# A decoder layer on one core: the v branch turned by transposing DMAs instead of TensorE

## The chip, the cores and the metric

The kernel runs on one core of one Trainium2 chip. The core has a matrix engine (TensorE, in the profile PE, its weight loads PEld), VectorE (DVE), ScalarE (ACT), GpSimd (POOL), and SyncE (SP), which here only issues DMAs. Each engine takes its instructions strictly in the order in which they were written; semaphores hold one back until what it needs is there. Times are device microseconds of one execution.

## What is computed

One layer of a decoder trunk over 1024 prompt tokens and 8 sample tokens, 1024 channels, all float32. The part that matters here is branch A:

```
u, v, z_a, x_b, z_b, g_a, g_b = split(rmsnorm(h) @ w_in)      # 7 x 1024 columns
vn  = layernorm(gelu(v))                    # over the 1024 channels of a token
s   = tril(w_s[g]) @ vn + b_s               # per chunk of 128 tokens, group of 128 channels
y_a = gelu(u) * s * silu(z_a)
```

The rest (a pooling branch B, a gated merge, an output projection, a second gate with a per-layer embedding) follows behind it and is not touched. Two of the outputs are rows of `vn`.

## The kernel before

**Products.** Every projection has its channels on the partitions and the tokens along the free axis, which is how `x` is kept. A *pair* is 256 output channels, so each of the seven branches has four pairs. A pair is computed by one step of Strassen's scheme: seven products of 12 matrix blocks (names P1 to P7, and in the profile by their operand: B11, T2, B21, T3, T4, T1, B22). Each float32 operand is split into a high half (ScalarE, a rounding copy) and a low half (VectorE, a subtraction), and a product takes three of the four combinations. So for every product ScalarE makes a weight half (`vw` for v, `gaw` for the gate branch), VectorE the other, and the results, in PSUM regions `acc`, are evacuated by ScalarE (`u<-acc`, `v<-acc`) or added by VectorE. Three such regions rotate. The order of branches is V, GA (gate), then U and ZA by turns, then branch B.

**The v branch.** A pair of v is two tiles `v` of 128 channels x 1032 tokens. LayerNorm runs over channels and the chunk mixing multiplies over tokens, so v is turned to tokens on the partitions, in `big[:, t, :]`, one row of 1024 channels per token block t. `v_turn` does that: PE transposes 128x128 blocks into a PSUM bank `vt` (two blocks t by two tiles, four at a time), and ScalarE reads the bank, applies the GELU, writes `big` and sums along the way (`vsums`). The sample tokens are the ninth block, `[S]`, into the tile `sv`. `V.turns` lists the blocks that are turned after each of the following products: five groups for a pair. The LayerNorm (`ln_stats`, `ln_apply`), the split of its result (`v_split`) and the mixing on PE (`spatial`, tile `mix`; for the sample tokens `sample_spatial`, tile `smix`) follow in the gate branch, one token block every four products.

**What sets the order.** The kernel is not written to the engines directly. A `Planner` records every operation with an estimated duration and the product that it belongs to (`at(step, f)` hangs an operation behind a product). It then orders each engine's queue by due times, and writes the result out (the one line L293, which is why all rows of the profile have that line). Weights are prepared three products ahead (`AHEAD`). 46 buffers of equal size (`slot`) are handed round among all tiles. DMAs other than the adding ones on POOL are issued from SP's queue, in the planned order.

Of the kernel before, what the change touches and what calls it, by code (L numbers as in the profile page):

```python
# [8 lines left out]
F32 = mybir.dt.float32  # L9
F32R = mybir.dt.float32r  # L10
BF16 = mybir.dt.bfloat16
AF = mybir.ActivationFunctionType
ALU = mybir.AluOpType

P = 128
D = 1024
NB = D // P
SEQ = 1024
NS = 8
# [35 lines left out]
class Planner:  # L55
# [24 lines left out]

    def space(self, ap):

        dims, start = list(ap.ap), ap.offset
        if "DRAM" in str(ap.space):
            row = ap.tensor.shape[-1]
            first, start = divmod(start, row)
            rows = sum(s // row * (n - 1) for s, n in dims if s >= row)
            return (ap.tensor.name, first, first + rows + 1,
                    ((start, start + sum(s * (n - 1) for s, n in dims if s < row) + 1),))
        row, parts = dims[0]  # L90
        first, start = divmod(start, row)
        pieces = [(start, start + 1)]
# [35 lines left out]
    def duration(self, engine, method, out, reads, kwargs):  # L128
        n = out.free_size()
        if engine == "tensor":  # L130
            return 0.109 if method == "transpose" else max(0.06, 0.0062 + n / 2268)
        if engine == "vector":
            if method == "tensor_reduce":
                n = reads[0].free_size()
            quick = method in ("tensor_scalar", "tensor_scalar_mul", "tensor_copy")
            quick = quick and self.tags.get(reads[0].tensor.name) in (None, "slot")
            return 0.065 + n * (0.00059 if quick else 0.00105) + (0.06 if method[:8] == "scalar_t" else 0)
        if engine == "scalar":
            return max(0.09 + n * 0.00086, 0.26 if n > 1 else 0) + (0.2 if kwargs.get("accum_out") is not None else 0)
        return 0.1 + n * 0.0008 if method == "memset" else 1.0  # L140

    def take(self, engine, method, args, kwargs):
        given = [*(("out" if i == 0 else "", a) for i, a in enumerate(args)), *kwargs.items()]
        writes = [a for k, a in given if k in ("out", "accum_out") and a is not None]
        reads = [a for k, a in given if k not in ("out", "accum_out") and hasattr(a, "tensor")]
        if kwargs.get("accum_op") is not None:
            reads += writes
        name = writes[0].tensor.name
        if engine == "tensor" and self.open is not None and self.open[0] == name:
            op = self.open[1]  # L150
        else:
# [5 lines left out]
        if method == "dma_start":  # L157
            op.busy, op.moved = 1.0 if engine == "gpsimd" else 0.45, writes[0].size() * 4e-6
# [141 lines left out]
def hybrid_step(  # L300
# [7 lines left out]
    nc = tc.nc  # L308
# [53 lines left out]
    ident = cpool.tile([P, P], F32, tag="ident", name="ident")  # L362
# [6 lines left out]
    nc = plan  # L369
# [3 lines left out]
    big = cpool.tile([P, NB, T], F32, tag="big", name="big")  # L373
# [34 lines left out]
    class Operand:  # L408
# [37 lines left out]
        def at(self, what, k):  # L446
            return [part[:, k % 2, :] for part in self.parts[what, k // 2]]
# [237 lines left out]
    class User:  # L685

        func = AF.Copy

# [165 lines left out]
            mul(quarter(kp, 1)[:, :, HALF:], ps[:, 2 * kp : 2 * kp + 2, :NS], g.to_broadcast([P, 2, NS]))  # L854

    S = NB
    xop = Operand("x")
    inp = lambda c0, i: w_in[:, c0 + 2 * i * P : c0 + (2 * i + 2) * P]


    NPAIR = NB // 2
    vsums = cpool.tile([P, NB + 1, NPAIR], F32, tag="vsums", name="vsums")
    sv = slot("sv", (P, D))
    vtok = lambda t: sv if t == S else big[:, t, :D]

    def v_turn(out, pair, ts):

        if ts == [S]:
            ps = bank("vt")
            for m in range(2):  # L870
                nc.tensor.transpose(ps[:NS, m * P : (m + 1) * P], out[m][:, SEQ:T], ident)
            places = [(S, ps[:NS, : 2 * P], NS)]
        else:
            ps = bank("vt").rearrange("p (t c) -> p t c", t=2)
            for i, t in enumerate(ts):
                for m in range(2):
                    nc.tensor.transpose(ps[:, i, m * P : (m + 1) * P], out[m][:, t * P : (t + 1) * P], ident)
            places = [(t, ps[:, i], P) for i, t in enumerate(ts)]
        for t, src, n in places:
            nc.scalar.activation(out=vtok(t)[:n, 2 * pair * P : (2 * pair + 2) * P], in_=src,  # L880
                                 func=AF.Gelu_apprx_tanh, accum_out=vsums[:n, t, pair : pair + 1])

    class V(User):
        turns = [[0, 1], [2, 3], [4, 5], [6, 7], [S]]

    lnv = {}

# [373 lines left out]
    at(vsteps[1][2], spatial_weights)  # L1261
    for i, u in enumerate(vusers):

        nxt = vsteps[1][3:] if i == 0 else (vsteps[i + 1][1:] if i + 1 < NPAIR else gasteps[0][0:])
        if i == 0:
            nxt = vsteps[1][2:]
        for s, ts in zip(nxt, V.turns):
            at(s, lambda u=u, i=i, ts=ts: v_turn(u.out, i, ts))
    at(vsteps[3][0], ln_rows)
    flow = [s for p in gasteps for s in p] + [s for p in usteps[0] for s in p]  # L1270
    for n, t in enumerate([NB - 1, *range(NB - 1)]):
        s = 3 + 4 * n
# [46 lines left out]
    turn_over(ybop, l, [*l[1:], c[0]])  # L1319


    rows = lambda t: NS if t == S else P
# [390 lines left out]
```

## Time and profile before

| | |
|---|---|
| three runs | 1001.23, 1001.62, 1002.43 us; median 1001.62 |
| profiled execution, span | 1002.0 us |
| PE busy | 989.1 us, 99% |
| VectorE, ScalarE, GpSimd busy | 800.1, 490.0, 73.7 us |
| granted clock of TensorE, mean | 0.996 |
| DMA | 166.95 MB, mean 167 GB/s |

The profiled execution and the median of the runs lie 0.4 us apart. V's products of pairs 1 to 3 run from 65 to 136 us, the gate branch from 131 us on. A row of a timeline gives start, length, engine and operation, as `out<-in`; a row of the waits gives who waited for whom: total, times, longest; a row of the windows gives a stretch and the busy time of PE, PEld, DVE, ACT and POOL in it, the granted clock, the DMA share and GB/s.

### The profile page before, as it was taken

The page shows a single profiled execution, that of the slowest core. Times are in us where ns is not written, and L with a number is a line of the kernel's source. Part 1 is how long each engine was busy: PE and PEld are TensorE (multiplying, and loading weights), DVE is VectorE, ACT ScalarE, POOL GpSimd, SP SyncE. Part 2 cuts the span into 40 slices and gives each one's busy share as a digit, 9 for nine tenths or more (in the row PEclk, how much of TensorE's full clock was granted, in tenths as well). Part 3 has the DMA queues.
Part 4 walks back from the last instruction along what each step waited for, and adds up shares of the span by engine and source line. Part 5 has one row for each costly group of instructions (what it writes and reads, how often), then busy time and mean ns, then how long its engine had stood idle before and what let it go on. Part 6 is the DMA issues. An engine that isn't in the chain of part 4 may idle for free.

```text
span 1002.0 us, 16159 instructions
## 1 busy us (share of the span) xinstructions
PE 989.1 (99%) x6200; PEld 889.8 (89%) x6200; DVE 800.1 (80%) x1241; ACT 490.0 (49%) x891; POOL 73.7 (7%) x162
## 2 busy tenths in 40 slices
PE   8999999999999999999999999999999999999996
PEld 7889999999999999999999999999999988888885
DVE  5985448877788788788898887697799798779796
ACT  7664356556434343233433343552353365677653
POOL 2200001000000000000000100000000002312111
PEclk9999999999999999999999999999999999999998
DMA  9231214222364345637544166884573553389546
GB/s 353 117 121 43 84 43 129 85 85 86 101 235 169 127 167 183 210 127 252 200 158 143 61 222 244 266 305 148 199 268 107 177 201 71 80 275 364 160 109 188
DMA packets 87330, 166.95 MB, mean 167 GB/s; under 512 B 7614, under 2 KB 47598, under 8 KB 87245
## 3 DMA queue, kind: packets, MB, share of 16 engines
q1 hardware_dynamic: 84885, 158.01, 45.3%
q0 software_dynamic: 2048, 7.37, 4.3%
q8 instruction: 49, 0.80, 0.3%
q10 hardware_dynamic: 320, 0.54, 0.2%
q14 instruction: 28, 0.23, 0.1%
HBM read 114.59 MB, written 51.77 MB: 166 GB/s over the span
## 4 chain that ended last, share of the span: by engine, by line
PE 97%; DVE 1%; POOL 0%; issue 0%; ACT 0%; POOLq 0%; DVEq 0%
PE acc L293 71%; PE acct L293 15%; PE accm L293 2%; PE e L293 2%; PE sps L293 2%; PE mix L293 1%; PE vt L293 1%; PE pst L293 1%; PE pht L293 1%; PE warm L293 1%; DVE sv L293 0%; DVE ge L293 0%; PE smix L293 0%; PE state L293 0%; DVE welo L293 0%
## 5 line engine op out<-in xcount | busy, mean ns | idle before, releaser
L293 DVE TENSOR_TENSOR u<-acc,u 128x520 f32<-128x520 f32 (+1 forms) x90 | 62.5, 695 | 36.5 <-PE acc L293 35.0
L293 POOL TENSOR_TENSOR rstd<-ms,mhalf 128x1 f32<-128x1 f32 (+1 forms) x45 | 38.2, 851 | 204.8 <-DVE ms L293 182.5
L293 POOL MEMSET u<- 128x8 f32 x35 | 3.5, 105 | 556.1 <-PE acc L293 242.5
L293 ACT ACTIVATE u<-acc 128x512 f32<-128x512 f32 x39 | 23.2, 596 | 33.4 <-PE acc L293 33.1
L293 ACT ACTIVATE paw<-pas 128x512 fp32r<-128x512 f32 x16 | 10.0, 627 | 30.0 <-DVE pas L293 24.8
L293 ACT ACTIVATE pbw<-pbs 128x512 fp32r<-128x512 f32 x16 | 10.0, 629 | 29.1 <-DVE pbs L293 25.9
L293 DVE TENSOR_TENSOR big<-big 128x1024 f32<-128x1024 f32 (+4 forms) x20 | 23.6, 1215 | 0.0
L293 ACT ACTIVATE big<-vt 128x256 f32<-128x256 f32 x32 | 11.9, 380 | 21.4 <-PE vt L293 21.4
L293 ACT ACTIVATE big<-pht,gvec 128x128 f32<-128x128 f32 x64 | 18.0, 381 | 8.0 <-PE pht L293 8.0
L293 ACT ACTIVATE big<-mix 128x256 f32<-128x256 f32 x32 | 12.1, 383 | 19.0 <-PE mix L293 18.6
L293 PE MATMUL accm<-qh,wpoolw 128*128 128x260 f32 (+1 forms) x96 | 21.0, 320 | 0.0
L293 ACT ACT_TABLE_LOAD x13 | 16.7, 1283 | 4.6 <-PE acc L293 3.6
L293 DVE TENSOR_TENSOR v<-acc,u 128x520 f32<-128x520 f32 (+1 forms) x9 | 6.3, 697 | 14.9 <-PE acc L293 14.8
L293 DVE TENSOR_TENSOR acc<-acc,u 128x512 f32<-128x512 f32 (+1 forms) x16 | 11.1, 697 | 8.7 <-PE acc L293 8.7
L293 ACT ACTIVATE gbw<-gbs 128x512 fp32r<-128x512 f32 x16 | 10.0, 624 | 16.4 <-DVE gbs L293 13.8
L293 ACT ACTIVATE zaw<-zas 128x512 fp32r<-128x512 f32 x16 | 10.0, 628 | 14.9 <-DVE zas L293 10.6
L293 ACT ACTIVATE zbw<-zbs 128x512 fp32r<-128x512 f32 x16 | 10.1, 630 | 14.6 <-DVE zbs L293 7.3
L293 PEld LDWEIGHTS accm<-qh,wpoolw 128*128 128x128 f32 x96 | 15.5, 188 | 1.9
L293 DVE TENSOR_TENSOR big<-mix,big 128x256 f32<-128x256 f32 x32 | 13.2, 421 | 4.4 <-ACT big L293 3.5
L293 ACT ACTIVATE uw<-us 128x512 fp32r<-128x512 f32 x16 | 9.8, 627 | 13.7 <-DVE us L293 7.2
L293 ACT ACTIVATE zbw<-zbraw 128x512 fp32r<-128x512 f32 x12 | 7.5, 626 | 18.2 <-DMA zbraw<-in_w_in_dram 9.2
L293 ACT ACTIVATE gb<-gb 128x1032 f32<-128x1032 f32 (+1 forms) x8 | 6.8, 854 | 18.8 <-DVE gb L293 18.8
(687 smaller groups left out, 3629.8 us busy)
## 6 DMA issues: line engine op xcount, KB each, us to landing
ga<-ga SPq DMA_DIRECT2D x16, 516.0 KB
gb<-gb SPq DMA_DIRECT2D x16, 516.0 KB
ya<-za SPq DMA_DIRECT2D x8, 516.0 KB
yb<-zb SPq DMA_DIRECT2D x8, 516.0 KB
x<-in_x_prompt_dram SPq DMA_DIRECT2D x8, 512.0 KB
vraw<-in_w_in_dram SPq DMA_DIRECT2D x8, 512.0 KB
e<-e SPq DMA_DIRECT2D x8, 512.0 KB
garaw<-in_w_in_dram SPq DMA_DIRECT2D x8, 512.0 KB
```

What stands on the lines that cost most here:

```text
L293: getattr(getattr(self.nc, e), method)(*args, **kwargs)
```

## The change

PE no longer turns the prompt tokens of v. Instead, for each tile, ScalarE copies the 1024 f32 values of a partition, seen as pairs of two-byte words, into two planes `vw` (all low words, all high words: two operations, `v_planes`). One transposing DMA from SP turns the 16 blocks of 128x128 words of these planes and writes them over the tile's own bytes (`v`). ScalarE then joins the words into f32 values in `big`, four token blocks in each of two operations (`v_join`). The GELU now reads `big` and writes it in place. The sample tokens are still transposed by PE. The planes are made behind the first of the following products, the joins behind the third and fourth, the GELUs behind the fifth to seventh (`V.turns`); the sample's turn moves from the last of these places to the first. LayerNorm and mixing move back by two products. The planner counts space in bytes and has durations for the new operations.

```diff
+    def v_planes(out, pair):
+
+        for m in range(2):
+            words, v = slot("vw", (P, 2, SEQ), U16), out[m][:, :SEQ].bitcast(U16)
+            for w in range(2):
+                nc.scalar.activation(out=words[:, w], in_=v.rearrange("p (t w) -> p w t", w=2)[:, w], func=AF.Copy)
+            nc.sync.dma_start_transpose(out=v.rearrange("p (k c) -> p k c", c=P),
+                                        in_=words.rearrange("p w t -> p (w t)"))
+
+    def v_join(out, pair, m):
+
+        c = 2 * (2 * pair + m) * P
+        for j in range(2):
+            ts = slice(4 * j, 4 * j + 4)
+            nc.scalar.activation(out=big.bitcast(U16)[:, ts, c : c + 2 * P].rearrange("p t (c w) -> p t c w", w=2),
+                                 in_=out[m][:, :SEQ].bitcast(U16).rearrange("p (w t c) -> p t c w", w=2, c=P)[:, ts],
+                                 func=AF.Copy)
+
     def v_turn(out, pair, ts):
 
         if ts == [S]:
             ps = bank("vt")
             for m in range(2):
                 nc.tensor.transpose(ps[:NS, m * P : (m + 1) * P], out[m][:, SEQ:T], ident)
-            places = [(S, ps[:NS, : 2 * P], NS)]
-        else:
-            ps = bank("vt").rearrange("p (t c) -> p t c", t=2)
-            for i, t in enumerate(ts):
-                for m in range(2):
-                    nc.tensor.transpose(ps[:, i, m * P : (m + 1) * P], out[m][:, t * P : (t + 1) * P], ident)
-            places = [(t, ps[:, i], P) for i, t in enumerate(ts)]
-        for t, src, n in places:
-            nc.scalar.activation(out=vtok(t)[:n, 2 * pair * P : (2 * pair + 2) * P], in_=src,
-                                 func=AF.Gelu_apprx_tanh, accum_out=vsums[:n, t, pair : pair + 1])
+        for t in ts:
+            n, c = rows(t), slice(2 * pair * P, (2 * pair + 2) * P)
+            v = vtok(t)[:n, c]
+            nc.scalar.activation(out=v, in_=ps[:NS, : 2 * P] if t == S else v, func=AF.Gelu_apprx_tanh,
+                                 accum_out=vsums[:n, t, pair : pair + 1])
 
     class V(User):
-        turns = [[0, 1], [2, 3], [4, 5], [6, 7], [S]]
+        turns = [[7, 0, 1], [2, 3, 4], [5, 6]]
...
     for i, u in enumerate(vusers):
 
-        nxt = vsteps[1][3:] if i == 0 else (vsteps[i + 1][1:] if i + 1 < NPAIR else gasteps[0][0:])
-        if i == 0:
-            nxt = vsteps[1][2:]
-        for s, ts in zip(nxt, V.turns):
-            at(s, lambda u=u, i=i, ts=ts: v_turn(u.out, i, ts))
+        nxt = vsteps[1][1:] + vsteps[2] if i == 0 else (vsteps[i + 1] if i + 1 < NPAIR else gasteps[0])
+        at(nxt[0], lambda u=u, i=i: v_turn(u.out, i, [S]))
+        at(nxt[0], lambda u=u, i=i: v_planes(u.out, i))
+        for m in range(2):
+            at(nxt[2 + m], lambda u=u, i=i, m=m: v_join(u.out, i, m))
+        for s, ts in zip(nxt[4:], V.turns):
+            at(s, lambda i=i, ts=ts: v_turn(None, i, ts))
...
-        s = 3 + 4 * n
+        s = 5 + 4 * n
```

ScalarE's queue around the first tile of pair 0 (`vw_298`, `vw_303` and so on are weight halves; `vt` is the bank that PE fills), before:

```order
L293 ACTIVATE vw_295<-vraw_279 128x512 [waits DMAHW4_49,DVE_49]
L293 ACTIVATE big,vsums<-vt_291 128x256 [waits PE_49]
L293 ACTIVATE big,vsums<-vt_291 128x256
L293 ACTIVATE vw_298<-vs_299 128x512 [waits DMAHW2_49,DVE_49,Activation_49]
L293 ACTIVATE vw_303<-vraw_280 128x512 [waits DMAHW5_49]
L293 ACTIVATE big,vsums<-vt_294 128x256 [waits PE_49]
```

and now (`v_213` is that tile, `vw_284` its planes, `vw_302` and `vw_298` weight halves):

```order
L297 ACTIVATE vw_284<-v_213 128x1024 [waits DMAHW2_49,DVE_49]
L297 ACTIVATE vw_284<-v_213 128x1024
L297 ACTIVATE wst_291<-psw_292 128x4x128 [waits PE_49,Pool_49]
L297 ACTIVATE vw_302<-vraw_280 128x512 [waits DMAHW2_49,DMAHW5_49,DMAHW1_49,PE_49]
L297 ACTIVATE big<-v_213 128x4x256 [waits DMAHW0_49]
L297 ACTIVATE vw_298<-vs_299 128x512 [waits DVE_49,Activation_49]
```

Where ScalarE waited for PE's transposes, its join now waits for a DMA, two instructions behind the planes, with the weight halves of pair 2 behind it.

ScalarE's queue at the turn from pair 2 to the gate branch, now (`v_314` and `v_315` are pair 2's tiles, `v_339` is pair 3's, `gaw_343` is the gate's first weight half):

```order
L297 ACTIVATE v_339<-acc_326 128x512 [waits PE_49]
L297 ACTIVATE big<-v_287 128x4x256
L297 ACTIVATE big<-v_288 128x4x256
L297 ACTIVATE big,vsums<-big 128x256 [waits Activation_49]
L297 ACTIVATE big<-v_314 128x4x256 [waits DMAHW6_49]
L297 ACTIVATE big<-v_314 128x4x256
L297 ACTIVATE big,vsums<-big 128x256 x4
L297 ACTIVATE big<-v_315 128x4x256 [waits DMAHW1_49]
L297 ACTIVATE gaw_343<-garaw_334 128x512 [waits DMAHW7_49,Activation_49]
```

Two joins that wait for their DMAs, and five GELUs, now stand ahead of the gate's first weight half, which before stood behind two GELUs.

SP's queue in the same part of the program, now (`vraw` are weights of pair 3, `garaw` those of the gate branch):

```order
L297 DMA_TRANSPOSE v_213<-vw_284 128x16x128 [waits DMAHW0_49,Activation_49]
L297 DMA_TRANSPOSE v_214<-vw_285 128x16x128 [waits DMAHW1_49,Activation_49]
L297 DMA vraw_309<-in_w_in_dram 128x4x256 [waits DMAHW2_49,DVE_49,Pool_49]
L297 DMA_TRANSPOSE v_287<-vw_307 128x16x128 [waits DMAHW3_49,Activation_49]
L297 DMA vraw_310<-in_w_in_dram 128x4x256 [waits DMAHW0_49,DMAHW4_49,DVE_49,PE_49]
L297 DMA_TRANSPOSE v_288<-vw_308 128x16x128 [waits DMAHW5_49,PE_49,Activation_49]
L297 DMA_TRANSPOSE v_314<-vw_329 128x16x128 [waits DMAHW6_49,DVE_49,Activation_49]
L297 DMA garaw_334<-in_w_in_dram 128x4x256 [waits DMAHW7_49,Pool_49]
L297 DMA garaw_335<-in_w_in_dram 128x4x256 [waits DVE_49,PE_49]
L297 DMA_TRANSPOSE v_315<-vw_330 128x16x128 [waits DMAHW1_49,Activation_49]
```

The loads, which before followed each other, now stand between transposing DMAs, each of which waits for ScalarE's planes.

More of the change, by code (lines that the diff above doesn't have):

```diff
@@ L11 @@
 BF16 = mybir.dt.bfloat16
+U16 = mybir.dt.uint16
 AF = mybir.ActivationFunctionType
@@ L81, in space @@
     def space(self, ap):
-        dims, start = list(ap.ap), ap.offset
+        size = 2 if ap.dtype in (BF16, U16) else 4
+        dims, start = [(s * size, n) for s, n in ap.ap], ap.offset * size
         if "DRAM" in str(ap.space):
-            row = ap.tensor.shape[-1]
+            row = ap.tensor.shape[-1] * size
             first, start = divmod(start, row)
@@ L88, in space @@
             return (ap.tensor.name, first, first + rows + 1,
-                    ((start, start + sum(s * (n - 1) for s, n in dims if s < row) + 1),))
+                    ((start, start + sum(s * (n - 1) for s, n in dims if s < row) + size),))
         row, parts = dims[0]
         first, start = divmod(start, row)
-        pieces = [(start, start + 1)]
+        pieces = [(start, start + size)]
         for s, n in reversed(dims[1:]):
@@ L138, in duration @@
         if engine == "scalar":
-            return max(0.09 + n * 0.00086, 0.26 if n > 1 else 0) + (0.2 if kwargs.get("accum_out") is not None else 0)
+            return max(0.09 + n * (0.00101 if out.dtype == U16 else 0.00086), 0.26 if n > 1 else 0) + (0.2 if kwargs.get("accum_out") is not None else 0)
+        if method == "tensor_copy":
+            return 0.15 + n * 0.0011
         return 0.1 + n * 0.0008 if method == "memset" else 1.0
@@ L156, in take @@
         op.spent.append(op.busy)
-        if method == "dma_start":
-            op.busy, op.moved = 1.0 if engine == "gpsimd" else 0.45, writes[0].size() * 4e-6
+        if method[:9] == "dma_start":
+            op.busy, op.moved = 1.0 if engine == "gpsimd" else 0.45, writes[0].size() * (2e-6 if writes[0].dtype == U16 else 4e-6)
             op.lands = 4.5 if kwargs.get("accum_op") is not None else 2.0
@@ L856, in hybrid_step @@
     S = NB
+    rows = lambda t: NS if t == S else P
     xop = Operand("x")
@@ L1319, in hybrid_step @@
     turn_over(ybop, l, [*l[1:], c[0]])
-    rows = lambda t: NS if t == S else P
     x_of = lambda t: x_sample if t == S else x_prompt[t * P : (t + 1) * P, :]
```

## The prediction

> **What bounds the kernel now.** The page first: busy time, slices, and the chain that ended last.
>
> ```profile
> span 1002.0 us, 16159 instructions
> PE 989.1 (99%) x6200; PEld 889.8 (89%) x6200; DVE 800.1 (80%) x1241; ACT 490.0 (49%) x891; POOL 73.7 (7%) x162
> PE   8999999999999999999999999999999999999996
> ACT  7664356556434343233433343552353365677653
> PE 97%; DVE 1%; POOL 0%; issue 0%; ACT 0%; POOLq 0%; DVEq 0%
> ```
>
> PE is busy in every slice and is 97% of the chain. A busy PE alone could be a PE that waits inside its instructions, so I read the waits of PE over the whole span: four, and after the start of the kernel only the last.
>
> ```profile
> PE warm L293 <- POOL ident masks.py:199: 1.9, 1, 1.9
> PE e L293 <- ACT wehi L293: 1.2, 1, 1.2
> PE e L293 <- DVE welo L293: 0.8, 1, 0.8
> PE smix L293 <- DVE sv L293: 0.2, 1, 0.2
> ```
>
> So PE's queue sets the end, instruction after instruction: work taken from it shortens the span by its own length, and a wait put into it lengthens the span by the wait's. The other engines count only where PE waits for them. In the V branch, which the change edits, ScalarE's slices (the fourth to the seventh, 75 to 175 us) read 3 to 6 tenths.
>
> **What is removed.** The chain of waits between 60 and 180 us, cut to the rows of the transposes `vt` and their neighbours (start, length, what):
>
> ```profile
> 69.83 5.64 PE acc L293 x36
> 79.38 0.59 PE vt L293 x4
> 79.97 2.79 PE acc L293 x12
> 82.75 0.44 PE vt L293 x4
> 83.19 2.90 PE acc L293 x24
> ...
> 92.62 0.22 PE vt L293 x2
> ...
> 146.32 0.44 PE vt L293 x4
> ```
>
> And the tile `vt` by itself, where each transpose reads 272 ns because it is pipelined with its neighbours:
>
> ```profile
> L293 PE MATMUL vt<-ident,v x72: 270/272/329, 79.3 to 149.5; 128*128 128x128 f32 x64, 128*8 128x128 f32 x8
> ```
>
> The price is therefore the 0.44 us that four of them hold the chain, not 4 x 0.272. The 64 full ones go, in 16 fours: 16 x 0.44 = **7.0 us**. The eight for the sample tokens (0.22 us a pair) stay. PE's order has 3674 rows before and 3610 now, so nothing takes their place there.
>
> **What is added, and what hides it.** ScalarE gets 16 splits into planes and 16 joins, each 1024 two-byte elements a partition; its 32 GELUs stay but read SBUF. Its order has two more table loads. SP gets eight transposing DMAs of 512 KB. Prices from ScalarE's timeline, where starts show what an instruction costs in a row of others:
>
> ```profile
> 66.11 1.05 ACT L293 ACTIVATE xT4h<-big 128x1024 fp32r<-128x1024 f32 x1
> 67.06 0.62 ACT L293 ACTIVATE vw<-vraw 128x512 fp32r<-128x512 f32 x1
> 80.00 0.39 ACT L293 ACTIVATE big<-vt 128x256 f32<-128x256 f32 x1 [1.95 <-PE vt L293]
> 80.28 0.20 ACT L293 ACTIVATION_READ_ACCUMULATOR big<-vt 128x1 f32 x1
> 80.38 0.38 ACT L293 ACTIVATE big<-vt 128x256 f32<-128x256 f32 x1
> 80.73 0.63 ACT L293 ACTIVATE vw<-vs 128x512 fp32r<-128x512 f32 x1
> 81.25 0.63 ACT L293 ACTIVATE vw<-vraw 128x512 fp32r<-128x512 f32 x1
> ```
>
> A copy of 1024 f32 elements takes 1.05 us and holds the engine 0.95 (66.11 to 67.06); a weight half 0.52 (80.73 to 81.25); a GELU with its sum 0.35 (80.38 to 80.73). No row copies two-byte elements. Below: 0.95. Above: a join writes four blocks of 256, and four separate 256-element activations of 0.38 make 1.52. It is one instruction of 1024, nearest to the first row; I take 1.1 for split and join.
>
> Then 32 x 1.1 = 35.2 us are added, and two table loads of 1.28 us, 2.6:
>
> ```profile
> L293 ACT ACT_TABLE_LOAD x13 | 16.7, 1283 | 4.6 <-PE acc L293 3.6 <-PEq L1700 0.8
> 75.00:100.00 25.00, 25.00 (x177) 22.99 (x176) 14.51 (x24) 12.06 (x38) 0.00 (x0) 1.00 0.14 43
> 100.00:125.00 25.00, 25.00 (x176) 23.25 (x175) 11.91 (x18) 9.81 (x33) 0.00 (x0) 1.00 0.25 85
> 125.00:150.00 25.00, 25.00 (x170) 22.79 (x169) 10.91 (x20) 13.37 (x38) 0.88 (x3) 1.00 0.13 43
> ```
>
> ScalarE (fifth column) is busy 12.06 + 9.81 + 13.37 = 35.2 of these 75 us. With 37.8 more it needs 73.0 in a stretch that shrinks to 68; the new order moves some 5 of it (eleven GELUs and the first LayerNorm square) further back. So ScalarE, with room to spare before, is nearly full, in strict order, and hides the work only if it is not also made to wait. Its waits for `vt` (1.95 us in the row at 80.00) go; in their place the first join of a tile waits for that tile's DMA, and weight halves and evacuations stand behind it.
>
> **How late a DMA may be.** Where an ordinary 512 KB load runs alone, SP issues it at 89.75 us, and its bytes stop soon after 93.0 (last two columns: DMA share, GB/s): 3.3 us. In a busy stretch one pair issued at 276.87 let ScalarE go at 281.98, 5.1 us. The longest 512 KB row is the adding load on POOL, 7.3.
>
> ```profile
> 89.75 3.40 SPq L293 DMA_DIRECT2D vraw<-in_w_in_dram  x2
> 92.00:93.00 1.00, 1.00 (x11) 0.95 (x10) 0.35 (x1) 0.13 (x1) 0.00 (x0) 1.00 0.76 268
> 93.00:94.00 1.00, 1.00 (x11) 1.00 (x10) 1.00 (x3) 0.86 (x3) 0.00 (x0) 1.00 0.11 17
> 276.87 0.93 SPq L293 DMA_DIRECT2D zaraw<-in_w_in_dram  x2
> 281.98 0.63 ACT L293 ACTIVATE zaw<-zaraw 128x512 fp32r<-128x512 f32 x1 [3.73 <-DMA zaraw<-in_w_in_dram]
> h<-in_x_prompt_dram POOLq DMA_DIRECT2D x8, 512.0 KB, 7.3
> ```
>
> No transposing DMA is in the trace: 3.3 below, 7.3 above. The DMA engines are a seventh to a quarter busy here, so I take 4 to 5. I walked ScalarE's new rows from the `wst` split (75.9 us) with the prices above, PE's products at 2.79 and 2.90. Two places decide. (a) Pair 3's first product is evacuated (`u`) behind the joins of pair 1; PE needs it before its third product, at 114.1 us. (b) The gate branch's first weight half (`gaw`) stands behind the joins of pair 2, and PE needs it, with VectorE's half 0.7 us later, at 128.3. With 4 us from issue to landing `u` is done at 108.6 and `gaw` is ready at 126: no wait, 2.4 us to spare. With 6 us the waits for the DMAs add up along the queue: (a) still holds, at (b) PE waits 2.0 us and at the next product 0.7. With 8 us it waits 4.1 at (a) and 5.9 at (b). Waiting begins near 5.2 us and grows by some 3.6 us for each further one.
>
> SP's other DMAs: the loads of pair 3's and the gate's weights now stand behind transposes that wait for ScalarE. In the walk pair 3's first load, behind the transpose of pair 0's second tile, issues at 92.6 (before at 89.75) and is used from 98; the gate's first at 116, used from 124. Both land in time.
>
> After the gate branch the LayerNorm steps come two products later, 2 x 2.85 = 5.7 us; their last use, pair 0 of ZA, keeps five products, so that costs nothing. From the U branch on the orders agree to the end, so what PE saves arrives there whole.
>
> The sum: 1002.0 - 7.0 = 995.0 us for the profiled execution, which lies 0.4 above the runs' median (1001.62). **Forecast: 994.6 us**, with waits at nothing.
>
> **Rivals.** (1) *ScalarE becomes the bound in the V branch.* The DMAs land after 6 us, or the joins cost 1.5: 16 x 0.4 = 6.4 us more ScalarE work, which uses up the 2.4 to spare and leaves 4. PE waits 3 to 4 us: 998. For it speaks the nearly full queue, against it the 3.3 us of a plain load.
> [...]
>
> (2) *The DMA takes the transposes' place as what PE waits for*: slower than before. At 7.3 us the waits are 3.6 x 2.1 = 7.6 us, more than the 7.0 gained. They also slow the clock:
>
> ```profile
> 158.42 1.92 PE smix L293 x16
> 160.34 7.37 PE acc L293 x36
> 161.00:162.00 1.00, 1.00 (x7) 1.00 (x6) 0.88 (x1) 0.00 (x0) 1.00 (x1) 0.50 0.41 169
> ```
>
> After the thin `smix` products the granted clock reads 0.50 and 36 products take 7.37 us where 5.64 is usual (69.83): 1.7 us. Two waits of about 4 us would cost that twice: 994.6 + 7.6 + 3.4 = 1005.6. The point is 6.2 us a DMA without the clock's part: 3.6 x 1.0 + 3.4 = 7.0. For it: the DMA moves 2-byte elements, and nothing here says that is as fast as rows of 1 KB. Against it: idle DMA engines.
> [...]
>
> (3) *More is gained.* The sample's last GELU now follows the gate's first product instead of its fifth, so `smix` waits for nothing (0.15 us before) and the slow clock behind it may not come: 994.6 - 1.7 - 0.2 = 992.7.
>
> **Numbers.** Forecast 0.53, (1) 0.20, (2) 0.18, (3) 0.09. Below 0.2% (2 us) a measurement of this kernel can't tell a difference. Faster: 0.53 + 0.09 + 0.13 of (1) = 0.75; same: 0.07 of (1) and 0.04 of (2) = 0.11; slower 0.14. The range goes from just under (3), 992, to 1003, inside (2); the likeliest case's own is 993.5 to 996.5.
>
> **What would show it.** Right: 64 fewer `vt` records, products of the V branch joining each other at 2.79 and 2.90, no new row among PE's waits, ScalarE at 9 tenths from 75 to 140 us, its waits for DMA under 2 us each. Wrong by (1): PE waiting for ScalarE at `vw` or `gaw` with joins over 1.4 us. Wrong by (2): ScalarE waiting 3 us or more for a DMA at several joins, PE idle near 114 and 128 us with the clock at half after it. If PE's waits are as forecast and the span is not, the order after the V branch is what I misread.

## The result

The changed kernel takes 1000.1 us, median of 19 executions (997.15 to 1002.76); the kernel before, run beside it, 1002.15 us (19 executions, 1001.19 to 1004.34). The ratio is **0.9975, with a 95% interval of 0.9965 to 0.9985**: 2 us faster, where 994.6 us and with it 7.0 were forecast. On two other chips the same kernel came to 0.9965 (0.9955 to 0.9976) and 0.9974 (0.9963 to 0.9984). Its executions spread over 5.6 us, with mean granted clocks of 0.993 to 0.998; the profiled one (span 995.8, reported time 997.51) is among the quickest, so the profile shows what the orders cost, and little of what the longer executions lose besides.

The page of that execution:

```profile
span 995.8 us, 16069 instructions
PE 981.3 (99%) x6136; PEld 881.0 (88%) x6136; DVE 800.5 (80%) x1241; ACT 526.0 (53%) x925; POOL 72.7 (7%) x162
PE   8999999999999999999999999999999999999996
ACT  7767888756434434243433343562353365677653
```

PE has 64 matmuls and 7.8 us of busy time less, ScalarE 36.0 us more (37.8 were forecast). PE is still the bound, but its waits are no longer only those of the start (total, times, longest):

```profile
PE warm L297 <- POOL ident masks.py:199: 1.9, 1, 1.9
PE acc L297 <- DVE v L297: 1.4, 1, 1.4
PE e L297 <- ACT wehi L297: 1.2, 1, 1.2
PE e L297 <- DVE welo L297: 0.8, 1, 0.8
PE acc L297 <- DVE u L297: 0.5, 1, 0.5
PE acc L297 <- DVE gaw L297: 0.3, 1, 0.3
PE pp L297 <- DMA p<-in_p_prompt_dram: 0.2, 1, 0.2
```

Three are new in the body: for `v`, `u` and `gaw`. The wait for `smix` is gone. The table of windows (busy us of PE, PEld, DVE, ACT, POOL; clock; DMA share; GB/s):

```profile
75.00:100.00 25.00, 25.00 (x173) 22.98 (x172) 14.68 (x24) 18.03 (x27) 0.00 (x0) 1.00 0.48 86
100.00:125.00 25.00, 25.00 (x167) 22.92 (x166) 10.09 (x16) 22.48 (x50) 0.11 (x1) 1.00 0.49 110
125.00:150.00 25.00, 23.14 (x155) 20.61 (x154) 16.86 (x30) 22.07 (x39) 0.87 (x3) 1.00 0.67 166
```

And two of ScalarE's groups (busy us and mean ns; the idle time ahead of them):

```profile
L297 ACT ACTIVATE big<-v 128x1024 uint16<-128x1024 uint16 x16 | 18.5, 1173 | 8.4 <-DMA v<-vw 8.4
L297 ACT ACTIVATE vw<-v 128x1024 uint16<-128x1024 uint16 x16 | 16.1, 1044 | 0.0
```

A split takes 1.04 us, a join 1.17. ScalarE is busy 62.6 of the 75 us, and its joins waited 8.4 us in all for the transposing DMAs. The DMA engines are two to five times as busy as before (shares of 0.48, 0.49 and 0.67 against 0.14, 0.25 and 0.13). The first transposing DMA stands alone, so its landing can be read: SP issues it at 79.37, and ScalarE, free from about 80.5, starts the join at 84.72, after 5.35 us.

```profile
79.37 1.72 SPq L297 DMA_TRANSPOSE v<-vw  x1
79.89 0.62 ACT L297 ACTIVATE vw<-vraw 128x512 fp32r<-128x512 f32 x1
84.72 1.18 ACT L297 ACTIVATE big<-v 128x1024 uint16<-128x1024 uint16 x1 [4.21 <-DMA v<-vw]
```

**Where the gain went.** PE's timeline at the turn from V to the gate branch, the first matmuls of each product:

```profile
122.43 0.40 PE L297 MATMUL acc<-xT1h,vw 128*128 128x260 f32 x2
126.86 0.51 PE L297 MATMUL acc<-xB22h,vw 128*128 128x260 f32 x2 [1.40 <-DVE v L297]
129.87 0.39 PE L297 MATMUL acc<-xB11h,gaw 128*128 128x512 f32 x1
132.96 0.38 PE L297 MATMUL vt<-ident,v 128*8 128x128 f32 x2
133.10 0.50 PE L297 MATMUL acc<-xT2h,gaw 128*128 128x260 f32 x2
136.67 0.39 PE L297 MATMUL acc<-xB21h,gaw 128*128 128x512 f32 x1
```

From start to start T1 takes 4.43 us, B22 3.01, B11 3.09 and T2 3.57: 14.1 where the four take 11.3 when nothing waits (2.87, 2.85, 2.75 and 2.87 at this place in a run below). So **2.8 us** are lost here, more than the 1.40 and 0.32 that the waits show. Three things stand behind it. VectorE and SP at the same time:

```profile
116.72 1.74 SPq L297 DMA_TRANSPOSE v<-vw  x1
118.55 1.76 SPq L297 DMA_DIRECT2D garaw<-in_w_in_dram  x2
120.41 4.90 SPq L297 DMA_TRANSPOSE v<-vw  x1
119.86 0.70 DVE L297 TENSOR_TENSOR u<-acc,u 128x520 f32<-128x520 f32 x1 [5.18 <-PE acc L297]
125.51 0.69 DVE L297 TENSOR_TENSOR gas<-garaw,garaw 128x512 f32<-128x512 f32 x1 [4.95 <-DMA garaw<-in_w_in_dram]
126.12 0.69 DVE L297 TENSOR_TENSOR v<-acc,u 128x520 f32<-128x520 f32 x1
```

The gate's first two loads, between two transposing DMAs, are issued from 118.55 on, and `gas`, which reads both, can start at 125.51, 7 us later. VectorE waits 4.95 us for them with `gas`, and behind `gas` stands `v<-acc,u`, which reads T1's sums. That PE has to wait for that reading is the second thing, an order of PE. Regions are numbered here; first the kernel before, then the changed one, a row for each product:

```
L293 MATMUL acc_353<-xT1h_260,vw_340 128x260 x2
...
L293 MATMUL acc_357<-xB11l_190,gaw_347 128x512
...
L293 MATMUL acc_353<-xB22h_231,vw_344 128x260 x2

L297 MATMUL acc_348<-xT1h_260,vw_338 128x260 x2
...
L297 MATMUL acc_348<-xB22h_229,vw_341 128x260 x2
...
L297 MATMUL acc_351<-xB11l_190,gaw_343 128x512
```

B22 accumulates onto the region that holds T1's sums, so VectorE has to have read them. Before, six transposes and the gate's B11 stood between; now B22 follows T1 directly, at this one place of the V branch: in the plan the gate's weights come too late for the order of before (asked for earlier, in a run below, they bring it back).

The third thing is on ScalarE:

```profile
127.34 1.19 ACT L297 ACTIVATE big<-v 128x1024 uint16<-128x1024 uint16 x1 [2.01 <-DMA v<-vw]
129.08 0.69 DVE L297 TENSOR_TENSOR gaw<-garaw,gaw 128x512 fp32r<-128x512 f32 x1 [1.67 <-ACT gaw L297]
```

A join that waits 2.01 us for its DMA stands ahead of ScalarE's half of the gate's first weights, and VectorE's half waits 1.67 us for that one. What is late by this falls on B11 and T2, which together take 1.0 us more than usual.

The third wait is far behind the change, at the end of a U pair:

```profile
323.12 1.22 DVE L297 TENSOR_TENSOR za<-za,big 128x1024 f32<-128x1024 f32 x1
324.26 1.42 DVE L297 TENSOR_TENSOR u<-acc,u 128x520 f32<-128x520 f32 x2
325.00 0.50 PE L297 MATMUL acc<-xB11h,zaw 128*128 128x512 f32 x1 [0.53 <-DVE u L297]
```

T1 of U begins at 321.44, so 3.56 us pass to 325.00 where 2.87 are usual: **0.7 us**. VectorE's order differs from the one before up to some 350 us, since the mixing ends two products later and the multiplications of ZA with it; on PE, T3 and T4 of this pair have changed places.

The two profiled executions now add up. 7.0 us are removed. 2.0 more are saved around `smix`: before, T2 behind it took 4.50 us and the product ahead of it 3.21, where 2.88 are usual. Of these 9.0, 2.8 and 0.7 are given back, which leaves 5.5, and that far apart the two are behind this place (the same B11 starts at 330.49 before and at 325.00 now); the spans differ by 6.2 (1002.0 and 995.8), and the other 0.7 come in the last few us. Without the slow clock that `smix` had in that execution of before, the gain is 7.0 - 3.5 = 3.5 us, and the quickest executions of both kernels lie 4.0 apart (1001.19 and 997.15).

### The profile page after: what moved, and what is told of

Read it like the earlier page. It is cut to its first block, busy times and chain, and to the rows that moved or that the text cites. A ratio compares the mean times of both kernels' runs of the same rounds, so it can differ in the third digit from the quotient of the medians.

```text
span 995.8 us, 16069 instructions
## 1 busy us (share of the span) xinstructions
PE 981.3 (99%) x6136; PEld 881.0 (88%) x6136; DVE 800.5 (80%) x1241; ACT 526.0 (53%) x925; POOL 72.7 (7%) x162
## 5 line engine op out<-in xcount | busy, mean ns | idle before, releaser
L297 DVE TENSOR_TENSOR u<-acc,u 128x520 f32<-128x520 f32 (+1 forms) x90 | 62.6, 696 | 38.8 <-PE acc L297 36.8
L297 ACT ACTIVATE big<-v 128x1024 uint16<-128x1024 uint16 x16 | 18.5, 1173 | 8.4 <-DMA v<-vw 8.4
L297 ACT ACTIVATE junk<-ge 128x512 bf16<-128x512 f32 (+2 forms) x19 | 11.6, 609 | 8.9 <-DVE ge L297 8.3
```

What stands on the lines that cost most here:

```text
L297: getattr(getattr(self.nc, e), method)(*args, **kwargs)
```

## The experiments

The theories changed on the way. At first: (A) the late load of the gate's weights makes PE wait; (B) the time is lost to a lower granted clock that has nothing to do with the change; (C) ScalarE is the bound, by its work or by its waits at the joins. After the first four runs: (D) PE's own order at the turn, B22 directly behind T1, is the loss, and (A) only lengthens it.

**Ordinary DMAs in place of the transposing ones.** The same 512 KB at the same places of SP's queue; v is not turned, so what follows computes on other numbers.

```diff
+                if method == "dma_start_transpose":
+                    method, kwargs = "dma_start", dict(kwargs, in_=kwargs["in_"].rearrange("p (k c) -> p k c", c=P))
```

> The eight transposing DMAs are ordinary DMA copies of the same 512 KB, from the planes over the same tile, in the same place of SP's queue; v is then not turned, so what stands behind it computes on other numbers. All splits, joins, GELUs and PE's products stay. Theory A (PE's wait comes from the gate's first load, which lands late because it shares the DMA engines and SP's queue with the transposing DMAs; VectorE waits for it ahead of the sum that frees PE's region): the copies hold SP under 1 us and land in about 3.5 us, the gate's load lands in time, PE's waits on v and gaw go, median 995 to 996.5 with all runs within 2 us. Theory B (the time was lost to a lower granted clock that has nothing to do with the transposing DMAs): median about 1000, with the same spread of 997 to 1003. Theory C (ScalarE is the bound, by the work of splits and joins): unchanged at 999 to 1000, since this work stays.

Measured 997.91 us, ratio to the kernel before 0.9946 (0.9935 to 0.9958). In its timelines:

```profile
79.63 0.54 SPq L299 DMA_DIRECT2D v<-vw  x1
83.22 1.19 ACT L299 ACTIVATE big<-v 128x1024 uint16<-128x1024 uint16 x1 [2.44 <-DMA v<-vw]
123.41 0.69 DVE L299 TENSOR_TENSOR gas<-garaw,garaw 128x512 f32<-128x512 f32 x1 [2.59 <-DMA garaw<-in_w_in_dram]
125.77 0.70 DVE L299 TENSOR_TENSOR v<-acc,u 128x520 f32<-128x520 f32 x1 [1.66 <-PE acc L299]
```

An ordinary DMA of these bytes holds SP 0.54 us instead of 1.72 and lands after 3.6 us instead of 5.35. VectorE now waits for the gate's load for 2.59 us and then for PE, so the load is in time. Its issue began at 116.46, 2.1 us earlier, and from there it took 6.95 us, as long as beside the transposing DMAs: it came late because it was issued late. Yet PE still waits 0.8 us for `v`: (A) explains 0.6 of the 1.4 us and no more. It was this run that led to (D).

**Joins that don't wait.** The joins read the planes instead of the turned tile; the DMAs still run. Again v is not turned.

```diff
+                if "in_" in kwargs and id(kwargs["in_"]) in self.swaps:
+                    kwargs = dict(kwargs, in_=self.swaps[id(kwargs["in_"])])
...
+            plan.swaps[id(turned)] = held[id(out[m])].rearrange("p w (t c) -> p t c w", c=P)[:, ts]
```

> The joins read the two planes instead of the turned tile, so ScalarE no longer waits for the transposing DMAs, which still run at the same places; v is then not turned, so what stands behind it computes on other numbers. Theory C (ScalarE's waits at the joins, 8.4 us in all, make PE wait): PE's waits on v, u and gaw go and the median is 995 to 996.5. Theory A (the late load of the gate's weights is what counts): ScalarE's 8.4 us go but VectorE's 5 us wait for garaw stays, PE's wait on v stays at 1 us or more, median 999 to 1000. Theory B: about 1000.

Measured 998.35 us, 0.9953 (0.9941 to 0.9965). ScalarE's 8.4 us of waiting at the joins are gone. PE's waits for `v` and `u` are as they were; the one for `gaw` is gone:

```profile
PE acc L299 <- DVE v L299: 1.4, 1, 1.4
PE acc L299 <- DVE u L299: 0.6, 1, 0.6
```

VectorE's half of the gate's first weights no longer waits for ScalarE:

```profile
127.55 0.68 DVE L299 TENSOR_TENSOR gaw<-garaw,gaw 128x512 fp32r<-128x512 f32 x1
```

B11 and T2 take 2.80 and 2.95 us instead of 3.09 and 3.57. So ScalarE's waits at the joins are not what PE's longest wait comes from, and (C) falls for it; but they cost 0.9 of the 2.8 us at the turn, and in other orders more (below).

**VectorE reads T1's sums first.** The sum `gas` is put behind the `v<-acc,u` that it stood ahead of.

```diff
...
+            held = calls.pop(i)
+            calls.insert(j, held)
...
```

> One instruction of VectorE moves: the sum gas of the gate's first weights, which waits for their load, now stands behind the addition v<-acc,u that it stood ahead of. Everything is computed. Theory A: PE's wait of 1.4 us for v goes; the wait moves to gaw or gaw's low half, where 1 us or less is left; with it the slower clock behind it goes in most runs; median 995.5 to 997.5. Theory B: no change, 1000 with a spread of 5 us. Theory C: no change, since ScalarE's queue is the same.

Measured 999.84 us, 0.9962 (0.9948 to 0.9977). The wait is shorter but stays:

```profile
128.28 0.51 PE L304 MATMUL acc<-xB22h,vw 128*128 128x260 f32 x2 [0.85 <-DVE v L304]
```

0.85 us are what VectorE needs to see T1's end, add (0.69) and let PE see it. But nothing is gained at the turn: B11 takes 3.74 us instead of 3.09, since VectorE's half of the gate's first weights comes no sooner (it waits 1.72 us for ScalarE's), and from T1 to the gate's B21 14.33 us pass, against 14.24 in the changed kernel. The mean granted clock of its profiled execution was 0.996 besides, against 0.998 in the changed kernel's. The expected 995.5 to 997.5 was missed.

**A later landing in the plan.** The planner is told 3.3 us for a transposing DMA instead of 2.0.

```diff
-            op.lands = 4.5 if kwargs.get("accum_op") is not None else 2.0
+            op.lands = 4.5 if kwargs.get("accum_op") is not None else 3.3 if method == "dma_start_transpose" else 2.0
```

> The planner is told that a transposing DMA lands 3.3 us after its bytes have gone, instead of 2.0, and orders the queues by that; everything is computed. The orders of ScalarE, VectorE and SP change in the V branch. Theory A: only if the gate's load is issued earlier or VectorE's waiting sum stands later does PE's wait go; I expect part of it, 997 to 999.5. Theory C (joins stand too early in ScalarE's queue): ScalarE's 8.4 us of waits at the joins fall to under 3 and the median goes to 995 to 997. Theory B: 1000.

Measured 998.18 us, 0.9955 (0.9943 to 0.9968). ScalarE waited for these DMAs at one join instead of four (4.0 us, and 2.5 at weight halves), the sum that waits for both halves of the gate's load stands behind the reading of T1's sums, and PE waits 0.8 us for `v`, with B11 and T2 behind them at 2.77 and 2.95 us instead of 3.09 and 3.57. A new wait of 0.6 us for a weight half `vw` comes. B22 still follows T1.

The turn as a whole, from T1's start to that of the gate's B21, takes 14.24 us in the changed kernel (13.7 to 14.1 in five more profiled executions of it), 13.29 with joins that don't wait, 12.89 with ordinary DMAs, 12.68 with the later landing, and 11.47 in the next run, where nothing waits. With the load and ScalarE in time, T1 and B22 still take 3.84 and 2.98 us instead of 2.87 and 2.85: 1.1 of the 2.8 us are the order's own. The other 1.7 hang on the late load and on ScalarE's late weight half: some 0.9 of them go when only ScalarE's waits go, none when only the sum `gas` is moved.

**Loads one product earlier.** This puts the gate's first load ahead of pair 2's transposing DMAs, and PE's order back to T1, B11, B22.

```diff
-    FETCH = 6
+    FETCH = 7
```

> All weights are asked for one product earlier (FETCH 7 instead of 6); the planner then issues the gate's first load ahead of pair 2's transposing DMAs and puts PE's products at the turn from V to the gate back into the order of before: T1, the gate's B11, then B22, which accumulates onto T1's region. Everything is computed. Theory D (formed after the first four runs: the loss at the turn comes from PE's own order; B22 now follows T1 directly and must wait until VectorE has read T1's sum out of the region, 0.8 us at least, 1.4 when the wait for the gate's load stands ahead of that reading): PE's wait for v goes, the excess of 2.7 us at the turn goes, span of an undisturbed execution near 993, median 995 to 997. If the remaining loss were the transposing DMAs' or ScalarE's (theories A and C), PE would now wait for gaw there instead, 1 us or more, and the median stay at 998 to 1000.

Measured 1004.94 us, 1.0023 (1.0013 to 1.0032): *slower* than the kernel before. At the turn (D) is right: T1, B11, B22 and T2 start at 122.35, 125.22, 127.97 and 130.82 and T2 ends at 133.69, one behind the other; there the 2.8 us are gained (the loads are earlier here too, so this run does not part the two). They are lost again 15 us later, on ScalarE and PE:

```profile
141.63 1.19 ACT L297 ACTIVATE big<-v 128x1024 uint16<-128x1024 uint16 x1 [3.46 <-DMA v<-vw]
142.72 1.14 ACT L297 ACTIVATE vh<-sv,npart 8x1024 fp32r<-8x1024 f32 x1
148.57 2.87 PE L297 MATMUL smix<-diag,sv 8*128 8x8 f32 x16 [2.75 <-DVE vsum L297]
```

and in the windows:

```profile
149.00:156.00 7.00, 7.00 (x35) 6.98 (x35) 3.41 (x9) 3.41 (x12) 0.00 (x0) 0.52 0.27 80
```

In this order a join that waits 3.46 us for its DMA stands ahead of the sample tokens' LayerNorm on ScalarE (`vh<-sv`). PE then waits 2.75 us for `smix`, and for the next 7 us its clock is at half: `smix` and the product behind it take 2.80 and 5.11 us instead of 1.88 and 2.88, another 3.1 us. Further on PE has new waits of 1.2 us for `zb`, 0.5 for `big` and 0.4 for `hw`. Together, 5.9 and 2.1 less 2.8, these are 5.2 of the 5.8 us by which the span (1001.6) exceeds the changed kernel's. The wait for `smix` is the prediction's second rival, at a place where it had not looked.

**The same, and VectorE's multiplication behind the evacuation at 321 us.**

```diff
...
+            i = hits[2]
+            j = next(j for j in range(i + 1, len(calls)) if calls[j][0] == "vector")
+            held = calls.pop(i)
+            calls.insert(j, held)
...
```

> As the run with loads one product earlier, and at 321 us one multiplication of VectorE (za<-za,big) is put behind the evacuation u<-acc that stood behind it and for which PE waited 0.5 us. Everything is computed. Theory D adds that the later mixing crowds VectorE in the U and ZA branches: another 0.5 to 0.7 us are gained, median 994.5 to 996.5, and PE has no wait after the start except 0.3 us. If that wait was an effect of the one ahead of it, it moves and nothing is gained against the other run.

Measured 1004.07 us, 1.0014 (1.0005 to 1.0022). The wait for `u` goes and one of 0.3 us for ScalarE's `zaw` comes; the wait for `smix` is 3.0 us.

**The changed kernel beside them.** No edit.

> The changed kernel itself, beside the others on the same chip: 997 to 1003, a median of about 1000, and the times in two groups, near 998 with a mean clock of 0.998 and near 1001.5 with 0.993 to 0.995. If the profiled execution is of the second group, its windows show where the clock is at half: theory D expects it behind PE's waits at the turn from V to the gate (127 to 140 us) or at the start; theory B has it anywhere.

Measured 998.94 us, 0.9965 (0.9955 to 0.9976). The profiled execution (clock 0.997) is at half clock at 11 to 14 us (3.4 us of it) and in the last few us, and nowhere behind the turn.

**The kernel before with PE's order of the changed one.** B22 of pair 3 directly behind T1 and its transposes; no transposing DMA.

```diff
...
+            last = [calls[i] for i in pe[after:end]]
+            for i in pe[after:end][::-1]:
+                del calls[i]
+            calls[pe[gate]:pe[gate]] = last
...
```

> The kernel before, with one change: PE's last product of V (B22 of pair 3) stands directly behind T1, ahead of the gate's first product. No transposing DMA. Everything is computed. Theory D: PE waits 0.8 us for VectorE's reading of T1's sum and the products behind it are slower; 1.0 to 1.5 us are lost against the kernel before, and if the slower clock follows such a wait, 2 to 4 us in a part of the executions. Theories A and C: no change, 1002, since neither DMAs nor ScalarE's work have changed.

Measured 1002.89 us, 1.0002 (0.9993 to 1.0011): no change, where (D) expected 1.0 to 1.5 us. PE and VectorE tell why:

```profile
129.74 0.81 PE L304 MATMUL vt<-ident,v 128*128 128x128 f32 x6
130.69 0.51 PE L304 MATMUL acc<-xB22h,vw 128*128 128x260 f32 x2
129.93 0.70 DVE L304 TENSOR_TENSOR v<-acc,u 128x520 f32<-128x520 f32 x1 [2.16 <-PE acc L304]
```

Six transposes, 0.95 us from 129.74 to 130.69, stand between T1 and B22, and VectorE reads T1's sums under them. In the kernel before the six hold PE 0.57 us, so some 0.4 us are lost to the reading here, too little for the medians to show. The order alone costs no more than that: it costs where the transposes that covered the reading are gone. The change removed the cover and swapped the products, and only both together make the whole wait.

**Row sums as the cover.** With the loads one product earlier, the row sums of the mixing weights (0.92 us on PE) are hung behind pair 3's T1.

```diff
-    FETCH = 6
+    FETCH = 7
...
-    at(flow[8], spatial_offsets)
+    at(vsteps[3][5], spatial_offsets)
```

> The loads one product earlier as before, and the row sums of the mixing weights (spatial_offsets, 0.92 us of PE work) are hung behind pair 3's T1 instead of nine products later, where PE's turn from V to the gate is. Everything is computed. The planner then keeps T1, row sums, B11, B22 and brings the sample's LayerNorm ahead again. Theory D: neither the wait for v at the turn nor the wait of 2.8 us for smix that the earlier loads alone brought; PE's waits after the start are under 1 us in all, and the slow stretch at 149 us goes; median 995 to 997, below both kernels. If the transposing DMAs themselves are too slow for this order (theory A, C), PE waits at smix or gaw for 1 us or more again, and the median is 999 or above.

Measured 1002.38 us, 1.0000 (0.9991 to 1.0009). T1, row sums, B11, B22 and T2 follow each other without a wait, but others come: 0.8 us for ScalarE's `v` at 124.68, and again `smix`:

```profile
149.33 1.21 DVE L297 TENSOR_TENSOR sv<-sv,lnb 8x1024 f32<-8x1024 f32 x1 [5.47 <-DMA lnb<-in_ln_b_dram]
150.60 1.95 PE L297 MATMUL smix<-diag,sv 8*128 8x8 f32 x16 [1.84 <-DVE sv L297]
```

This time VectorE waits 5.47 us for `lnb`, a parameter of the LayerNorm whose load stands behind two transposing DMAs in SP's queue and is issued at 143.60. Behind the wait for `smix` the clock is at half until 157 us. Each order without the loss at the turn has had one at `smix`.

**The dose doubled.** The changed kernel, with the gate's first two loads behind the next transposing DMA.

```diff
...
+            held = calls.pop(turn)
+            calls.insert(gate[0], held)
...
```

> The changed kernel with the dose doubled: the gate's first two loads are issued behind the next transposing DMA, which holds SP 4.9 us, instead of ahead of it. Everything is computed. Theory D (VectorE's wait for the load stands ahead of its reading of T1's sum, which PE waits for): VectorE's wait grows from 5 to about 10 us, PE's wait for v from 1.4 to 5 to 6.5 us; and as the smix wait of 2.8 us did in the run with earlier loads, a wait that long brings half the clock for several us behind it: median 1005 to 1009. If the clock is not lowered by the wait, 1003 to 1005. If PE's wait does not hang on that load, 1000.

Measured 1003.95 us, 1.0023 (1.0012 to 1.0033). VectorE and PE in the timeline:

```profile
130.66 0.69 DVE L303 TENSOR_TENSOR gas<-garaw,garaw 128x512 f32<-128x512 f32 x1 [7.70 <-DMA garaw<-in_w_in_dram]
131.27 0.69 DVE L303 TENSOR_TENSOR v<-acc,u 128x520 f32<-128x520 f32 x1
132.11 0.77 PE L303 MATMUL acc<-xB22h,vw 128*128 128x260 f32 x2 [4.24 <-DVE v L303]
```

and the windows:

```profile
130.00:138.00 8.00, 5.89 (x27) 5.84 (x28) 4.62 (x8) 4.04 (x10) 0.00 (x0) 0.57 0.44 167
```

VectorE's wait grows by 2.75 us and PE's by 2.84, so the chain load, `gas`, `v<-acc,u`, PE is shown. And here the clock falls behind the wait: B22 takes 5.33 us, 2.5 more than usual. 2.8 + 2.5 = 5.3 us against a measured 5.0 above the 998.94 of the changed kernel on another chip; since this profiled execution has half the clock behind `smix` too, from 158 to 162 us, that the two agree so closely is partly chance. The size was somewhat under the expected 1005 to 1009, as PE's wait was under the expected 5 to 6.5.

**The best of the orders, mended at 321 us.** The later landing, and the multiplication behind the evacuation.

```diff
-            op.lands = 4.5 if kwargs.get("accum_op") is not None else 2.0
+            op.lands = 4.5 if kwargs.get("accum_op") is not None else 3.3 if method == "dma_start_transpose" else 2.0
...
+            held = calls.pop(i)
+            calls.insert(j, held)
...
```

> The transposing DMA's landing planned 3.3 us after its bytes, as in the earlier run of that kind, and at 321 us VectorE's multiplication za<-za,big put behind the evacuation u<-acc for which PE waited 0.7 us. Everything is computed. Theory D: the waits on v at the turn (0.8 us, with little behind it) stay, the one at 321 us goes; 0.3 to 0.7 us less than with the landing alone, 997 to 998.5, and 0.5 to 2 us less than the changed kernel on the same chip. If the waits have little to do with the time that is left, it equals the changed kernel.

Measured 997.91 us, 0.9959 (0.9947 to 0.9972), with the changed kernel on the same chip at 999.15 and 0.9974 (0.9963 to 0.9984). The two intervals overlap: it is ahead of the kernel before, but not shown to be ahead of the changed one. The wait for `u` went, and one of 0.5 us for `zaw` came. Its profiled execution shows something else (windows):

```profile
10.00:15.00 5.00, 4.24 (x12) 3.14 (x12) 4.39 (x8) 5.00 (x9) 1.87 (x3) 0.66 1.02 393
150.00:155.00 5.00, 5.00 (x20) 4.14 (x20) 4.62 (x14) 4.64 (x9) 0.46 (x1) 0.66 0.11 36
```

The second stretch is the product behind `smix`, which PE did not wait for: 4.45 us instead of 2.8.

**Where the longer executions lose.** The changed kernel again, without an edit; the first is the one of the 999.15 us.

> The changed kernel once more beside it: 997 to 1003. A profiled execution with a mean clock of 0.995 or less would show the slow stretches of its longer executions: theory D expects one right behind PE's wait for v at 127 us, besides those at the start (11 us) and behind smix (150 us).

> A single look at the changed kernel. If its mean clock is 0.996 or less: theory D has a stretch of half the clock at 127 to 135 us, behind PE's wait for v; theory B has none there, but one at 11 us or behind smix at 150 us.

> A second look at the changed kernel, with the same expectations: half the clock behind PE's wait for v (theory D), or only at the start and behind smix (theory B).

> A third look at the changed kernel, with the same expectations: half the clock behind PE's wait for v (theory D), or only at the start and behind smix (theory B).

The profiled execution of the first (clock 0.998) has half the clock in its last 3 us alone. The others took 997.35, 997.87 and 998.37 us, with waits of 1.0 to 1.3 us for `v` at the turn; one has half the clock at 10 to 13 us, and none has it behind the turn. None of the profiled executions of the changed kernel had a mean clock under 0.997, while single ones of the timed executions had 0.993. Of the 19 executions of the result, nine have spans of 995.4 to 996.7 us and ten of 998.4 to 1001.1; of the ten, eight have clocks of 0.993 to 0.995, but two 0.997, as quick ones have, so the clock need not be all of it. Where the longer ones lose their 3 to 5 us **stays open**. Half the clock was seen at the start, behind `smix` with and without a wait, behind waits of 1.8 us and more, and in the last 3 to 6 us of the spans, where PE has no work left; of the turn in the changed kernel it was only argued.

## Why the prediction was wrong

The direction was right, the size was not: 2.05 us came of 7.0. Point by point:

- **What bounds the kernel, and what is removed: right.** PE still sets the end; 64 matmuls are gone and the products of the V branch join each other.
- **ScalarE's work: right in sum.** 1.04 and 1.17 us an operation where 1.1 was taken, 36.0 us where 37.8 were. It was busy for 62.6 of the 75 us, where the forecast had it nearly full.
- **The DMA, 4 to 5 us from issue to landing: a little short.** 5.35 us alone. The forecast that no wait for it would reach 2 us failed (4.21 and 2.01). PE did not pay for the first; for the one of 2.01, ahead of the gate's first weight half, it paid 0.9 us, as the run with joins that don't wait showed. The walk put the gate's first half at 126 for 4 us; it was ready at 129.0.
- **"Both land in time": failed.** The gate's first load was walked to ScalarE's use only, with an issue at 116; it was issued at 118.55. VectorE used it first, waited 4.95 us, and held the evacuation behind it: 0.6 us of PE's wait, by the run with ordinary DMAs.
- **"PE's order has 3674 rows before and 3610 now, so nothing takes their place there": the step that failed most.** It is a count, not an order. B22 and B11 had changed places, and the transposes taken out had been the cover under which VectorE read T1's sums. With the late load and ScalarE's late weight half it cost 2.8 us at the turn, the largest term that the sum lacked; 1.1 of them are its own. The walk asked when each operand must be *there*, never when a region must be *read*.
- **"From the U branch on the orders agree to the end": failed.** VectorE's order differs to about 350 us, and PE's at one pair of U; 0.7 us.
- **The sum's base.** Span and reported time are not the same measure: the changed kernel's profiled execution has a span of 995.8 and a reported time of 997.51. Set beside the median as if they were, before's profiled span looked 0.4 above it. From the reported median of 1002.15 the 7.0 us lead to 995.2, not 994.6.
- **The rivals.** (1) came in small part: no join cost 1.5 us and ScalarE did not become the bound, but the 0.9 us at the turn came through its waiting joins. A join took 1.17 us in this trace, 0.13 more than a split (1.04). (2) was the right mechanism at the wrong place: it came whole in the runs with earlier loads, with a wait of 2.75 us and 3.1 of slow clock, and made them slower than before. (3) came in the profiled execution (no wait for `smix`, the products behind it without a slow clock), but in the run at 0.9959 the clock fell behind `smix` without any wait (0.66 from 150 to 155 us), so it is no steady gain.
- The forecast's 4 of 7 us in the quickest executions, and 2 of 7 in the median: the remaining 2 us are the longer executions, most of them with a lower clock, which the forecast had no term for; where they lose it is open.

## What to carry to other kernels

An instruction that is taken out may be the cover of another engine's work: before a term is written as "removed", look at what runs under it (here VectorE's reading of a region that the next product writes), and at the order of the instructions around the gap, not at their number. Where a planner sets the order, any edit of durations, space or places moves work far from the edit; compare the orders of every engine to the end, and walk each transfer to the first engine that waits for it, with what stands behind the waiting instruction. A wait of PE can cost more than its length: 5.9 us for 2.75 at `smix`, where the clock fell behind it; and the list of waits can show less than is lost, 1.7 of 2.8 us at the turn.

## What the runs showed of the hardware

- **A transposing DMA was dearer than a copy here, and it held the queue.** The first 512 KB within SBUF landed 5.35 us after the issue, against 3.6 for an ordinary DMA of the same bytes at the same place, so it took one and a half times as long; the eight held SP's queue for 1.49 to 4.90 us, against 0.46 to 0.65. The gate's loads, once issued, took 7 us beside transposing DMAs and 6.95 beside ordinary ones, so these runs do not show that it slows its neighbours in any other way.
- **Ahead of the last few us, the slow clock came in pieces of 3.4 us, or of twice that.** Summing (1 - clock) over the 1-us windows and dividing by 0.5 gives 3.4 us at half clock for the stretch at 160 us of the kernel before, 3.4 for both stretches of the run at 0.9959, and 6.8 behind the waits of 2.75 us (earlier loads) and 4.24 us (dose doubled). The same kernel has such a piece in one execution and not in another: of the six profiled executions of the changed kernel two have 3.4 us of it between 10 and 15 us, and the other four none there. Nor was a wait needed: in the run at 0.9959 the clock is at half behind the 16 thin `smix` products of 1.9 us, ahead of which PE did not wait. What sets the length, and when a piece begins, these runs do not show.
